# One filling quantum fewer behind each read-back of inverses, and one tile and one cadence for the modulation sums through the border, both branch projections and the output projection

## The chip, the cores and the metric

The kernel runs on one core of a Trainium2 chip. The metric is the device time of one execution in microseconds (us); of several runs the median counts.

## The reference

One layer of a bidirectional hybrid encoder, 256 tokens, width 2048, everything in f32:

```python
mod = c_act @ ada_w + ada_b                      # c_act = silu(c); six parts of 2048
shift_m, scale_m, gate_m, shift_f, scale_f, gate_f = split(mod, 6)
h = rms_norm(x) * (1 + scale_m) + shift_m
proj = h @ w_in                                  # q,k,v,gates of two branches, merge gates
y_a = (sigmoid(a_o) * rms_norm(mLSTM both ways)) @ w_branch_a
y_b = (rms_norm(gated delta rule both ways) * silu(b_z)) @ w_branch_b
x = x + gate_m * ((g_a * y_a + g_b * y_b) @ w_out)
hf = rms_norm(x) * (1 + scale_f) + shift_f
x = x + gate_f * ((silu(hf @ w_gate) * (hf @ w_up)) @ w_down)
return rms_norm(x) * norm_final_w
```

The gated delta rule (GDN) has 16 heads. For each chunk it needs the inverse of a unit triangular matrix. The mLSTM has 4 heads.

## The kernel before, in words

**Products.** Each weight is loaded as f32 (`raw`), and split into a high part `wh` (ScalarE, ACT) and a low part `wl` (VectorE, DVE, `wl = raw - wh`). TensorE (PE) adds three products. A `tjob` (line 197) makes 512 output columns: eight *quanta*, each one half (`k0`) of a 1 MB load `raw`, with one `wh`, one `wl` and 12 matmuls of 512 columns. An `fjob` (line 173) makes 128 output columns in two quanta of 24 matmuls of 256. `raw`, `wh` and `wl` have three buffers each, so the split of a quantum runs two quanta ahead of PE.

**Filling.** `rest` (line 392) lists projection jobs that nothing urgent waits for: `v`, then `mb`, `o`, `a`, `ma` groups 0 to 3. `fill(n)` issues n quanta of the list. They are set between the links of the GDN chains, whose matmuls are short and wait for one another.

**GDN.** Heads go in four groups g of four. `invert(g)` makes the inverses of a group on DVE (`gdn_invert`, lines 704 and 710, tiles `uu`, `utmp`), stores them to DRAM (`inv_d`, line 696, issued by POOL), and `gdn_blocks` reads them back as `cg` (line 723, POOL). The main loop then issues `fill(8)` (line 1029), so that the filling covers this trip, and next the transposition of `cg` (line 725) and the mixing into `R` (lines 729, 730) on DVE. `gdn_phase2` handles two heads at once in nine steps; the last ones are the output product `po` (lines 829 to 834), the normalization `on` (squares on ACT, line 857; root, line 862; DVE, lines 858 to 868) and the transposition `px` on PE (line 841), which ACT copies to `obt` (line 845) and stores to DRAM (`ob_d`, line 846). For the pair p = 1 of group 3 `px` ends the GDN part.

**Border.** Then the memory of the GDN part is given free. `o_load` (line 1076) reads the four groups of `ob_d` back, `o_split` makes `obh` and `obl` (lines 1080, 1081). The first two mLSTM heads (`cores`) run their denominators `pden` (line 962) and numerators `ph` (line 978). Next come the projection of branch B (`y_b`, tiles `yb`) with the two other heads between its quanta, that of branch A (`y_a`, tiles `ya`), and the output projection (`o_job`, tiles `o`, four groups g of 512 columns). In `o_job(3)` the last quarter is done token by token (`by_token`, lines 257 to 259), since its end releases the second norm.

**Modulation sums.** Parts 2 to 5 of `mod` are 16 sums each. `ask` (line 111) loads a 1 MB row tile `ada` on SP's queue, `add` (line 120) is one DVE instruction of 128 x 2048 (line 124) with the sum as its accumulator. Parts 2, 3 and 4 (48 sums) start with the first GDN group; part 4 (`scale_f`) is needed at the end of the output projection for `affn` (line 1313). `pump` (line 157), called once a quantum, sets them: with `room` of one tile it adds when the tile was asked for more than two quanta ago and a sum is owed (every `every[0]` quanta), and asks for the next a quantum later, so that with `every` at 1 a sum comes each four quanta; `held` keeps sums off the first steps of a pair. With `room` of three tiles (pool `sr`) each owed sum is one call of `sums`, which first fills all three tiles and then adds one.

Before, `every` is 0 from the border until the last two mLSTM heads, 1 there, and 4 with three tiles in `y_a`. In `o_job` it is 0, and `sums()` is called after quanta (4, 7), (2, 5), (2, 5) and (0, 2) of the four groups; after quantum 4 of the last one `sums(P)` adds all that are left.

Of the kernel before, what the change touches and what calls it, by code (L numbers as in the profile page):

```python
# [9 lines left out]
F32 = mybir.dt.float32  # L10
# [5 lines left out]
P = 128  # L16
T = 256
D = 2048
# [34 lines left out]
def hybrid_block(ctx: ExitStack, tc: tile.TileContext, xr, nfr, crow, pk_d, cst_d, ada2, ada4, win0, winb, wint, wba, wbb, wo, wgu, wd, out, dbg=None):  # L53
# [3 lines left out]
    def pool(stack, name, bufs=1, **kw):  # L57
        return stack.enter_context(tc.tile_pool(name=name, bufs=bufs, **kw))
# [3 lines left out]
    rows_p = pool(ctx, "rows")  # L62
# [9 lines left out]
    def order(ins, yes=True):  # L72

        return tc.keep_in_program_order(ins) if yes else ins
# [30 lines left out]
        order(S.activation(row_c[:, g * 512 : (g + 1) * 512], pc_, AF.Silu))  # L105


    room = [(rows_p, "ada", 1, 1)]
    asked, unasked, age = [], [], [0]

    def ask():

        pl, tag, bufs, _ = room[0]
        part, b = unasked.pop(0)
        raw = pl.tile([P, D], F32, tag=tag, bufs=bufs, name=f"ada{part}_{b}")
        order(nc.sync.dma_start(raw, ada4[part - 2, b]))
        asked.append((part, b, raw))
        age[0] = 0

    def add():  # L120

        part, b, raw = asked.pop(0)
        c = part * KB + b
        order(V.scalar_tensor_tensor(raw, raw, 1.0, row_c[:, :D], ALU.mult, ALU.mult, accum_out=mod[:, c : c + 1]))  # L124
        if b == KB - 1:
            c = slice(part * KB, part * KB + KB)
            V.tensor_tensor(mod[:, c], mod[:, c], pk[:, PK_ADAB + c.start : PK_ADAB + c.stop], ALU.add)
# [11 lines left out]
    def settle(keep=0, only=None):  # L139

        now = [f for f in behind if only is None or f.__name__ == only]
        for f in now[: len(now) - keep]:
            behind.remove(f)
            f()

    count, every = [0], [0]
    owed, held = [0], [False]

    def sums(n=1):

        while n and (unasked or asked):
            while unasked and len(asked) < room[0][3]:
                ask()
            add()
            n -= 1

    def pump():
        count[0] += 1
        age[0] += 1
        if every[0] and count[0] % every[0] == 0:  # L160
            owed[0] = 1
        if room[0][3] > 1:
            if owed[0]:
                owed[0] = 0
                sums()
        elif asked:
            if owed[0] and age[0] > 2 and not held[0]:
                owed[0] = 0
                add()
        elif unasked and every[0]:  # L170
            ask()
# [97 lines left out]
    def fill(n=1):  # L269

        while n and fills:
            if next(fills[0], None):
                n -= 1
            else:
                fills.pop(0)
# [217 lines left out]
    with ExitStack() as s0:  # L493
# [35 lines left out]
        ra, raw = loads(0)  # L529
# [18 lines left out]
        for b in range(KB):  # L548
            if b:
                ra, raw = loads(b)  # L550
# [475 lines left out]
    for g in range(4):  # L1026
        blocks = gdn_blocks(g)
        next(blocks)
        fill(8)
        next(blocks)  # L1030
        fill(1)
        pairs = [gdn_phase2(g, p) for p in range(2)]
        if g == 3:
            settle()
            sf.close()
            mq["pool"] = pool(sq_, "mq", side="right")
            first2 = [mlstm(h) for h in range(2)]
            for c in first2:
                next(c)
        every[0] = 1  # L1040
        for p in range(2):
            pieces = stream(4 * g + 2 * p + 4)
            for n in range(1, 10):

                held[0] = n < 4
                if p == 0:
                    next(blocks, None)
                next(pairs[p], None)
                if g == 3 and n == (8, 4)[p]:
                    next(first2[p])  # L1050
                for _ in range(last[n] if g == 3 else second[n] if p else after[n]):
                    next(pieces)
            for _ in pairs[p]:
                pass

            if g < 3:
                while 4 * g + 2 * p + 5 not in heads:
                    next(pieces)
        if g < 3:
            fills.insert(0, z_job(g + 1))  # L1060
            every[0] = owed[0] = 0
            invert(g + 1)
# [55 lines left out]
            yield from y_b(g)  # L1118

    o4s = [o_load(g) for g in range(2)]  # L1120
    every[0] = owed[0] = 0
    cores = steps(*first2)
    fill(1)
    next(cores)
# [19 lines left out]
    o_split(3, o4s[3])  # L1144
    fill(2)
    drive(cores, 3)
    every[0] = 1
    drive(steps(mlstm(2), mlstm(3)), 3)
    fill(1000)
    mgh, mgl = big(bigC, F32R, "mgh"), big(bigC, F32R, "mgl")  # L1150
    sm_.close()
    sr_ = ExitStack()
    if asked:
        add()
    room[0] = (pool(sr_, "sr"), "sr", 3, 3)
    gm = room[0][0].tile([P, D], F32, name="gm")
    dgs = {}

    def row_diag(part, g, rp):
        ms = mods[:, part == 5]  # L1160
        if not g:
            m = mod[:, part * KB : (part + 1) * KB]
            V.tensor_copy(ms[:, 0], m)
            V.tensor_tensor(ms[:, 1], m, ms[:, 0].bitcast(F32), ALU.subtract)
        dg = dgs[part, g] = rp.tile([P, 2, 4, P], F32R, tag="dg", bufs=2, name=f"dg{part}_{g}")
        for i in range(2):
            V.tensor_tensor(
                dg[:, i], ident.unsqueeze(1).broadcast_to([P, 4, P]),
                ms[:, i, 4 * g : 4 * g + 4].bitcast(F32).unsqueeze(2).broadcast_to([P, 4, P]), ALU.mult,
            )  # L1170
# [6 lines left out]
            PE.matmul(pr, onesr, woven(dg[:, i]), start=i == 0, stop=i == 1)  # L1177
        S.activation(woven(dst[:, g * 512 : (g + 1) * 512]), pr.rearrange("p (c h) -> p c h", h=2), AF.Copy)

    every[0] = 4  # L1180
    for g in range(4):
        for i, _ in enumerate(y_a(g)):
            if g and i == 3:
                merged(g - 1, mgh, mgl)
            if i in (1, 5) and g < 2:
                row_diag(2, 2 * g + i // 4, room[0][0])
            if i in (3, 7) and g < 2:
                row_spread(2, 2 * g + i // 4, gm)
    every[0] = 0


    def o_job(g, front=None):
# [112 lines left out]
    for g in range(4):  # L1305
        if g == 3:
            root()
        for i, _ in enumerate(o_job(g, front_o if g == 3 else None) if g else o_first, 0 if g else 2):
            if i in ((4, 7), (2, 5), (2, 5), (0, 2))[g]:
                sums()  # L1310
            if g == 3 and i == 4:
                sums(P)
                V.scalar_tensor_tensor(
                    affn, mod[:, 4 * KB : 5 * KB], 1.0, pk[:, PK_NFFN : PK_NFFN + KB], ALU.add, ALU.mult
                )
    if dbg is not None and "x1" in dbg:
        G.dma_start(dbg["x1"], x1)
    room[0] = (rows_p, "ada", 1, 1)
    ada_parts(5)
    sw.close()  # L1320
    sr_.close()
# [73 lines left out]
    for j in range(FB // 4):  # L1395
# [4 lines left out]
        for e2 in range(2):  # L1400
            px = gps(f"pxf{j}_{e2}")
            for e in range(2):
                f = 2 * e2 + e
                for t in range(2):
                    PE.transpose(px[:, e * T + t * P : e * T + (t + 1) * P], sg[:, t, f * P : (f + 1) * P], ident)
            b = 4 * j + 2 * e2
# [156 lines left out]
```

## Time and profile before

| what | us |
|---|---|
| median of 3 runs (1970.23 to 1975.39) | 1972.22 |
| the profiled execution's own time | 1972.89 |
| its span, first to last instruction | 1970.8 |
| PE busy in the span | 1929.8 |
| DVE busy | 1405.4 |
| ACT busy | 1025.8 |

The profile is of one execution. Its times count from the span's start. A matmul's end is modelled and overlaps the next one's start, so a busy PE is read by when its matmuls start. An f32 matmul with f32 operands stands as two records.

### The profile page before, as it was taken

To read this page: it belongs to the slowest core of one execution; us is meant where nothing else is said; L and a number is where in the kernel's file an instruction comes from. 1 tells how busy PE (TensorE), PEld (TensorE's weight loads), DVE (VectorE), ACT (ScalarE), POOL (GpSimd) and SP (SyncE) were. 2 spreads that over 40 slices of the span, in tenths; PEclk is the share of its full clock that TensorE was granted. 3 is DMA by queue.
4 is the path that set the end of the run, shared out by engine and by line. 5 is a ranking of instruction groups with operands and counts; after the bars stand their busy time and mean duration, and the time that the engine had idled before them with its cause. 6 is when DMAs were issued, how large, how long until landed. Compare 5 with 4: busy or idle time off the path is not lost.

```text
span 1970.8 us, 27090 instructions
## 1 busy us (share of the span) xinstructions
PE 1929.8 (98%) x10418; PEld 1705.2 (87%) x10418; DVE 1405.4 (71%) x2067; ACT 1025.8 (52%) x1551; POOL 116.6 (6%) x211
## 2 busy tenths in 40 slices
PE   8999999999999999999999999999999999999998
PEld 6878889998999899889787888788888888888886
DVE  6779886887788788866577878866665665555554
ACT  3137646765776577565534444644444444444444
POOL 0001210111011101110100000200000000000000
PEclk9999999999999999999899999999999999999999
DMA  9987676667576766686776888576676665565553
GB/s 399 420 349 233 182 255 241 217 221 235 213 219 214 243 209 219 208 293 244 242 296 247 343 301 333 206 255 236 241 268 239 235 239 207 195 214 199 207 199 143
DMA packets 78962, 485.64 MB, mean 246 GB/s; under 512 B 10585, under 2 KB 15969, under 8 KB 24433
## 3 DMA queue, kind: packets, MB, share of 16 engines
q1 hardware_dynamic: 63216, 450.69, 62.6%
q0 software_dynamic: 8160, 17.88, 4.4%
q10 hardware_dynamic: 7458, 15.36, 2.0%
q8 instruction: 81, 1.33, 0.3%
q14 instruction: 47, 0.39, 0.1%
HBM read 467.07 MB, written 16.82 MB: 246 GB/s over the span
## 4 chain that ended last, share of the span: by engine, by line
PE 85%; DVE 6%; DMA 5%; ACT 2%; issue 1%; SPq 0%; ACTq 0%; DVEq 0%
PE acc_gt L234 4%; PE acc_gt L235 4%; PE acc_gt L236 4%; PE acc_up L234 4%; PE acc_up L235 4%; PE acc_up L236 4%; PE acc_d L234 4%; PE acc_d L236 4%; PE acc_d L235 4%; DMA ra<-ada 3%; PE acc_b L187 2%; PE acc_b L189 2%; PE acc_o L236 2%; PE acc_b L188 2%; PE acc_o L234 2%; PE acc_o L235 2%
## 5 line engine op out<-in xcount | busy, mean ns | idle before, releaser
L215 DVE TENSOR_TENSOR wl_d<-raw_d,wh_d 128x1024 fp32r<-128x1024 f32 x88 | 107.7, 1224 | 105.9 <-ACT wh_d L213 105.9
L215 DVE TENSOR_TENSOR wl_up<-raw_up,wh_up 128x1024 fp32r<-128x1024 f32 x88 | 107.6, 1224 | 100.2 <-ACT wh_up L213 100.1
L215 DVE TENSOR_TENSOR wl_gt<-raw_gt,wh_gt 128x1024 fp32r<-128x1024 f32 x88 | 108.1, 1229 | 79.4 <-ACT wh_gt L213 79.4
L187 PE MATMUL acc_b<-hh,wh_b 128*128 128x256 f32 x576 | 162.8, 283 | 0.0
L189 PE MATMUL acc_b<-hh,wl_b 128*128 128x256 f32 x576 | 159.4, 277 | 0.1
L188 PE MATMUL acc_b<-hl,wh_b 128*128 128x256 f32 x576 | 159.1, 276 | 0.0
L213 ACT ACTIVATE wh_d<-raw_d 128x1024 fp32r<-128x1024 f32 x88 | 92.9, 1056 | 126.3 <-PE acc_d L235 118.9
L213 ACT ACTIVATE wh_gt<-raw_gt 128x1024 fp32r<-128x1024 f32 x88 | 92.9, 1056 | 121.2 <-PE acc_gt L235 71.0
L213 ACT ACTIVATE wh_up<-raw_up 128x1024 fp32r<-128x1024 f32 x88 | 92.8, 1056 | 108.1 <-PE acc_up L235 77.1
L124 DVE SCALAR_TENSOR_TENSOR ada<-ada,crow 128x2048 f32<-128x2048 f32 x64 | 145.9, 2283 | 0.0
L234 PE MATMUL acc_gt<-wh_gt,hfh 128*128 128x512 f32 x352 | 135.9, 386 | 0.0
L235 PE MATMUL acc_gt<-wh_gt,hfl 128*128 128x512 f32 x352 | 135.1, 384 | 0.0
L236 PE MATMUL acc_gt<-wl_gt,hfh 128*128 128x512 f32 x352 | 134.2, 381 | 0.0
L234 PE MATMUL acc_up<-wh_up,hfh 128*128 128x512 f32 x352 | 133.4, 379 | 0.0
L235 PE MATMUL acc_up<-wh_up,hfl 128*128 128x512 f32 x352 | 133.4, 379 | 0.0
L236 PE MATMUL acc_up<-wl_up,hfh 128*128 128x512 f32 x352 | 133.4, 379 | 0.0
L234 PE MATMUL acc_d<-wh_d,ffh 128*128 128x512 f32 x344 | 130.5, 379 | 0.0
L235 PE MATMUL acc_d<-wh_d,ffl 128*128 128x512 f32 x344 | 130.5, 379 | 0.0
L236 PE MATMUL acc_d<-wl_d,ffh 128*128 128x512 f32 x344 | 130.4, 379 | 0.0
L561 PE MATMUL first<-x,raw 128*128 128x256 f32 x512 | 114.5, 382 | 7.4 <-ACT x L555 7.0
L561 PEld LDWEIGHTS first<-x,raw 128*128 128x128 f32 x512 | 96.0, 190 | 25.9 <-ACT x L555 12.6
L188 PEld LDWEIGHTS acc_b<-hl,wh_b 128*128 128x128 f32 x576 | 111.3, 193 | 0.1
(382 smaller groups left out, 5262.1 us busy)
## 6 DMA issues: line engine op xcount, KB each, us to landing
ada<-ada SPq DMA_DIRECT2D x64, 1024.0 KB, 6.2
raw_gt<-wgu SPq DMA_DIRECT2D x44, 1024.0 KB, 4.9
raw_up<-wgu SPq DMA_DIRECT2D x44, 1024.0 KB, 4.9
raw_d<-wd SPq DMA_DIRECT2D x44, 1024.0 KB, 4.9
raw_b<-winb SPq DMA_DIRECT2D x36, 1024.0 KB, 5.0
ra<-ada SPq DMA_DIRECT2D x32, 1025.0 KB, 15.6
raw<-win SPq DMA_DIRECT2D x16, 1024.0 KB, 14.5
raw_z<-wint SPq DMA_DIRECT2D x16, 1024.0 KB, 5.2
```

What stands on the lines that cost most here:

```text
L124: order(V.scalar_tensor_tensor(raw, raw, 1.0, row_c[:, :D], ALU.mult, ALU.mult, accum_out=mod[:, c : c + 1]))
L187: PE.matmul(o, wh[:, k], woven(hh[:, kk]), start=kk == 0, stop=False)
L188: PE.matmul(o, wh[:, k], woven(hl[:, kk]), start=False, stop=False)
L189: PE.matmul(o, wl[:, k], woven(hh[:, kk]), start=False, stop=kk == KB - 1)
L213: order(S.activation(wh, raws[u][:, k0 : k0 + 2], AF.Copy), early)
L215: order(V.tensor_tensor(wl, raws[u][:, k0 : k0 + 2], wh.bitcast(F32), ALU.subtract), early)
L234: order(PE.matmul(ps[t], xh[:, kk, c], woven(wh[:, k]), start=kk == 0, stop=False), early and steps > 1)
L235: PE.matmul(ps[t], xl[:, kk, c], woven(wh[:, k]), start=False, stop=False)
L236: PE.matmul(ps[t], xh[:, kk, c], woven(wl[:, k]), start=False, stop=kk == last)
L561: PE.matmul(first[o], raw[:, o], x[:, b], start=b == 0 and o % 2 == 0, stop=b == KB - 1 and o % 2 == 1)
```

## The change

Three things change, all in the order of the work; every product and every sum is still made.

1. After the read-back of groups 1, 2 and 3 seven quanta are issued in place of eight. What is not issued there comes later from the same list.
2. The three-tile pool `sr` for the sums goes: `room` goes, and all 48 sums go through the one tile of `rows_p`. `every` stays at 1 from GDN group 3 on, through the border (where `held` is set to false), `y_b`, `y_a` and `o_job`. The calls of `sums()` after single quanta go.
3. What is left of part 4 is summed after quantum 3 of `o_job(3)`, not after quantum 4.

```diff
-    room = [(rows_p, "ada", 1, 1)]
     asked, unasked, age = [], [], [0]
 
     def ask():
 
-        pl, tag, bufs, _ = room[0]
         part, b = unasked.pop(0)
-        raw = pl.tile([P, D], F32, tag=tag, bufs=bufs, name=f"ada{part}_{b}")
+        raw = rows_p.tile([P, D], F32, tag="ada", name=f"ada{part}_{b}")
...
         while n and (unasked or asked):
-            while unasked and len(asked) < room[0][3]:
+            if not asked:
                 ask()
             add()
...
-        if room[0][3] > 1:
-            if owed[0]:
-                owed[0] = 0
-                sums()
-        elif asked:
+        if asked:
             if owed[0] and age[0] > 2 and not held[0]:
...
-        fill(8)
+        fill(7 if g else 8)
         next(blocks)
         fill(1)
...
     o4s = [o_load(g) for g in range(2)]
-    every[0] = owed[0] = 0
+    held[0] = False
     cores = steps(*first2)
...
     drive(cores, 3)
-    every[0] = 1
     drive(steps(mlstm(2), mlstm(3)), 3)
...
-    if asked:
-        add()
-    room[0] = (pool(sr_, "sr"), "sr", 3, 3)
-    gm = room[0][0].tile([P, D], F32, name="gm")
+    sr = pool(sr_, "sr")
+    gm = sr.tile([P, D], F32, name="gm")
...
-    every[0] = 4
     for g in range(4):
         for i, _ in enumerate(y_a(g)):
...
-    every[0] = 0
...
         for i, _ in enumerate(o_job(g, front_o if g == 3 else None) if g else o_first, 0 if g else 2):
-            if i in ((4, 7), (2, 5), (2, 5), (0, 2))[g]:
-                sums()
-            if g == 3 and i == 4:
+            if g == 3 and i == 3:
+                every[0] = owed[0] = 0
                 sums(P)
...
-    room[0] = (rows_p, "ada", 1, 1)
     ada_parts(5)
```

The order in which the two programs issue their instructions shows what this does. The lines of the changed kernel are lower by 6 (lines 184 to 1100), by 11 in the residual code and by 2 in `add`.

**First place: DVE at the read-back of group 2** (`uu` ends the inversion, `cg` is the read-back, `wl_o` and `wl_b` are low parts of quanta). Before:

```order
L710 TENSOR_TENSOR uu_4939<-uu_4939,utmp_5937 64x30
L215 TENSOR_TENSOR wl_o_0_2_6342<-raw_o_0_6323,wh_o_0_2_6341 128x1024
L215 TENSOR_TENSOR wl_o_1_0_6360<-raw_o_1_6357,wh_o_1_0_6359 128x1024
L215 TENSOR_TENSOR wl_o_1_2_6376<-raw_o_1_6357,wh_o_1_2_6375 128x1024
L215 TENSOR_TENSOR wl_o_2_0_6394<-raw_o_2_6391,wh_o_2_0_6393 128x1024
L215 TENSOR_TENSOR wl_o_2_2_6410<-raw_o_2_6391,wh_o_2_2_6409 128x1024
L215 TENSOR_TENSOR wl_o_3_0_6428<-raw_o_3_6425,wh_o_3_0_6427 128x1024
L725 STREAM_TRANSPOSE cg_6296<-cg_6296 128x512
```

The same place on DVE after the change:

```order
L704 TENSOR_TENSOR uu_4908<-uu_4908,utmp_5919 64x30
L209 TENSOR_TENSOR wl_o_0_0_6326<-raw_o_0_6323,wh_o_0_0_6325 128x1024
L209 TENSOR_TENSOR wl_o_0_2_6342<-raw_o_0_6323,wh_o_0_2_6341 128x1024
L209 TENSOR_TENSOR wl_o_1_0_6360<-raw_o_1_6357,wh_o_1_0_6359 128x1024
L209 TENSOR_TENSOR wl_o_1_2_6376<-raw_o_1_6357,wh_o_1_2_6375 128x1024
L209 TENSOR_TENSOR wl_o_2_0_6394<-raw_o_2_6391,wh_o_2_0_6393 128x1024
L719 STREAM_TRANSPOSE cg_6278<-cg_6278 128x512
L723 TENSOR_SCALAR R<-cg_6278,cst 128x256
```

Between the inversion's last instruction and the transposition stand five low parts in place of six.

**Second place: PE at the end of the GDN part** (`po`, `px` of the last two heads, `acc_ma` the last job of `rest`). Before, `po` comes after the last quantum of the list, and `px` right behind it:

```order
L236 MATMUL acc_ma_1_9102<-wl_ma_3_2_9289,hh 128x512
L829 MATMUL po_1_9310<-z_1_9208,at_7688 128x128
...
L834 MATMUL po_1_9310<-z_1_9208,at_7987 128x128
L841 MATMUL px_1_9311<-cst,on_1_0_9324 128x128 x2
L962 MATMUL pden_9374<-ones,mdec_8891 128x1
L841 MATMUL px_1_9311<-cst,on_1_1_9325 128x128
L962 MATMUL pden_9374<-ones,mdec_8891 128x1 x5
```

After the change three quanta (`ma_2_2`, `ma_3_0`, `ma_3_2`) stand between `po` and `px`; this is the end of the last one and what follows:

```order
L229 MATMUL acc_ma_1_9137<-wh_ma_3_2_9322,hl 128x512
L230 MATMUL acc_ma_1_9137<-wl_ma_3_2_9323,hh 128x512
L835 MATMUL px_1_9257<-cst,on_1_0_9270 128x128 x2
L835 MATMUL px_1_9257<-cst,on_1_1_9271 128x128 x2
L956 MATMUL pden_9375<-ones,mdec_8798 128x1 x6
L956 MATMUL pden_9392<-ones,mdec_9088 128x1 x6
L972 MATMUL ph_0_0_9411<-vt_8808,mdec_8798 128x512
```

On DVE, a little later, a sum now stands in the border, behind the last `obl` and ahead of a low part of `yb` (after the change):

```order
L209 TENSOR_TENSOR wl_yb_1_2_9529<-raw_yb_1_9508,wh_yb_1_2_9528 128x1024
L1075 TENSOR_TENSOR obl<-o_3_9429,obh 128x1024
L122 TENSOR_SCALAR ada_8_9490,mod<-ada_8_9490,crow 128x2048
L209 TENSOR_TENSOR wl_yb_2_0_9548<-raw_yb_2_9545,wh_yb_2_0_9547 128x1024
L979 RECIPROCAL ssh_9406<-ssh_9406 128x2
```

Before, one `hs` of line 987 (128x512) stood there in place of the sum; that `hs` comes later now.

**Third place: DVE in the last group of the output projection** (`ada_12` to `ada_15` are sums of part 4). Before:

```order
L215 TENSOR_TENSOR wl_o_1_0_11464<-raw_o_1_11461,wh_o_1_0_11463 128x1024
L124 TENSOR_SCALAR ada_12_11376,mod<-ada_12_11376,crow 128x2048
L215 TENSOR_TENSOR wl_o_1_2_11483<-raw_o_1_11461,wh_o_1_2_11482 128x1024
L215 TENSOR_TENSOR wl_o_2_0_11501<-raw_o_2_11498,wh_o_2_0_11500 128x1024
L124 TENSOR_SCALAR ada_13_11442,mod<-ada_13_11442,crow 128x2048
L124 TENSOR_SCALAR ada_14_11479,mod<-ada_14_11479,crow 128x2048
L124 TENSOR_SCALAR ada_15_11516,mod<-ada_15_11516,crow 128x2048
L215 TENSOR_TENSOR wl_o_2_2_11524<-raw_o_2_11498,wh_o_2_2_11523 128x1024
L127 TENSOR_TENSOR mod<-mod,pk 128x16
L215 TENSOR_TENSOR wl_o_3_0_11542<-raw_o_3_11539,wh_o_3_0_11541 128x1024
```

After the change:

```order
L209 TENSOR_TENSOR wl_o_1_0_11468<-raw_o_1_11465,wh_o_1_0_11467 128x1024
L209 TENSOR_TENSOR wl_o_1_2_11484<-raw_o_1_11465,wh_o_1_2_11483 128x1024
L122 TENSOR_SCALAR ada_14_11447,mod<-ada_14_11447,crow 128x2048
L209 TENSOR_TENSOR wl_o_2_0_11508<-raw_o_2_11505,wh_o_2_0_11507 128x1024
L209 TENSOR_TENSOR wl_o_2_2_11524<-raw_o_2_11505,wh_o_2_2_11523 128x1024
L209 TENSOR_TENSOR wl_o_3_0_11542<-raw_o_3_11539,wh_o_3_0_11541 128x1024
L122 TENSOR_SCALAR ada_15_11500,mod<-ada_15_11500,crow 128x2048
L209 TENSOR_TENSOR wl_o_3_2_11546<-raw_o_3_11539,wh_o_3_2_11545 128x1024
L125 TENSOR_TENSOR mod<-mod,pk 128x16
```

Two of the sums stand earlier now, and the last one has the last two low parts around it. With one tile its load can be issued only when `ada_14` has been added; on SP's queue it stands behind the load of `raw_gt_0`.

More of the change, by code (lines that the diff above doesn't have):

```diff
@@ L1185, in hybrid_block @@
             if i in (1, 5) and g < 2:
-                row_diag(2, 2 * g + i // 4, room[0][0])
+                row_diag(2, 2 * g + i // 4, sr)
             if i in (3, 7) and g < 2:
                 row_spread(2, 2 * g + i // 4, gm)
-    every[0] = 0
     def o_job(g, front=None):
```

## The prediction

> **What bounds the kernel now.** I read the page first: busy times, then the waits of PE, then the chain of waits where they lie.
>
> ```profile
> PE 1929.8 (98%) x10418; PEld 1705.2 (87%) x10418; DVE 1405.4 (71%) x2067; ACT 1025.8 (52%) x1551; POOL 116.6 (6%) x211
> PE 85%; DVE 6%; DMA 5%; ACT 2%; issue 1%; SPq 0%; ACTq 0%; DVEq 0%
> ```
>
> PE is busy for 98% of the span and holds 85% of the chain. The change takes no matmul away, so it can only gain where PE stands still or runs at a lower clock. The waits of PE (us in total, times, longest) name two such places that the change touches:
>
> ```profile
> PE acc_o L236 <- DVE wl_o L215: 3.7, 4, 2.1
> PE px L841 <- DVE on L868: 3.6, 1, 3.6
> ```
>
> The second is the end of the GDN part. The chain there (start, us, what), the clock of three stretches (us, then busy PE, PEld, DVE, ACT, POOL, then the granted clock, DMA share, GB/s), and three rows of the same chain elsewhere:
>
> ```profile
> 951.54 0.24 PE po L834 x2
> 951.80 1.14 ACT on L857 x8
> 953.20 1.06 issue
> 955.40 0.73 PE px L841 x2
> 956.67 2.35 PE pden L962 x12
> 959.34 1.93 PE pden L962 x10
> 961.26 12.66 PE ph L978 x24
> 973.92 0.22 PE acc_yb L234
> ```
>
> ```profile
> 950.00:962.00 12.00, 8.37 (x45) 7.70 (x45) 2.88 (x9) 4.57 (x14) 0.00 (x0) 0.73 0.32 126
> 962.00:966.00 4.00, 4.00 (x6) 1.61 (x5) 0.59 (x6) 0.93 (x3) 2.59 (x4) 0.54 0.71 243
> 1022.00:1031.00 9.00, 9.00 (x47) 7.93 (x46) 5.17 (x11) 2.46 (x4) 0.00 (x0) 0.81 0.85 303
> ```
>
> ```profile
> 994.64 0.87 PE pxa L994 x8
> 1023.37 2.57 PE pden L962 x24
> 1035.51 5.15 PE ph L978 x12
> ```
>
> PE ends `po` at 951.78 and starts `px` at 955.40: it waits 3.62 us for squares, root and normalization. Behind the wait it runs at a lower clock (0.73, then 0.54). `px` and 24 `pden` take 5.86 us from 955.40 to 961.26; at full clock eight transpositions take 0.87 and 24 `pden` 2.57, 3.44 in all. The 24 `ph` take 12.66 against 2 x 5.15 = 10.30. So from `po` to the first matmul of `yb` 22.14 us pass, where 13.74 would do if nothing had to be waited for.
>
> **The change, part by part.** (a) **Border.** Three quanta, one saved behind each read-back, now stand between `po` and `px`. A quantum's pitch is seen from two low parts on DVE, one after the other:
>
> ```profile
> 674.05 1.23 DVE L215 TENSOR_TENSOR wl_o<-raw_o,wh_o 128x1024 fp32r<-128x1024 f32 x1 [1.37 <-ACT wh_o L213]
> 676.64 1.22 DVE L215 TENSOR_TENSOR wl_o<-raw_o,wh_o 128x1024 fp32r<-128x1024 f32 x1 [1.36 <-ACT wh_o L213]
> 678.71 0.71 DVE L725 STREAM_TRANSPOSE cg<-cg 128x512 f32<-128x512 f32 x1 [0.84 <-DMA cg<-inv_d]
> 680.35 1.22 DVE L215 TENSOR_TENSOR wl_o<-raw_o,wh_o 128x1024 fp32r<-128x1024 f32 x1
> ```
>
> It is 2.59 us, so the three last 7.8. What they must cover is the 3.62 of before, and what may stand ahead of the normalization on DVE now, one sum (2.28, below) and one low part (1.22): 7.1 at most. So the wait goes whole, and with it, as I take it, the low clock behind it: 3.62 + (5.86 - 3.44) + (12.66 - 10.30) = 8.40.
>
> A gap that closes shows what is late next. `yb` needs `obh` and `obl`, which come from DRAM:
>
> ```profile
> 959.37 0.84 ACT L845 ACTIVATE obt<-px,pk 128x256 f32<-128x256 f32 x2 [4.82 <-PE px L841]
> 962.63 1.51 POOL L1076 DMA_DIRECT2D o<-ob_d  x2 [55.44 <-ACT dn L964]
> 972.95 0.76 POOL L1076 DMA_DIRECT2D o<-ob_d  x1 [0.80 <-DVE obl L1081]
> 979.95 1.23 DVE L1081 TENSOR_TENSOR obl<-o,obh 128x1024 fp32r<-128x1024 f32 x1 [0.75 <-ACT obh L1080]
> 981.76 1.22 DVE L215 TENSOR_TENSOR wl_yb<-raw_yb,wh_yb 128x1024 fp32r<-128x1024 f32 x1
> ```
>
> This trip is DMA after DMA on POOL's queue (store, two loads, two more when the first are split), and a faster PE doesn't shorten it: from `obt` at 959.37 to the end of the last `obl` at 981.18 it takes 21.8. Count from the start T of `px` in the changed kernel. `obt` follows two evictions of `ma` on ACT, at about T + 1.1, so the last `obl` ends at T + 22.9. Behind it now stand the sum `ada_8` (2.28) and then the low part of quantum 4 of `yb` (1.22): T + 26.4. PE is at that low part's first product at T + 13.74 + 4 x 2.59 + 0.43 = T + 24.5. It waits 1.9. Net gain of the border 8.40 - 1.9 = **6.5**, with 8.4 as one end (trip shorter, no wait) and 3 as the other (the trip or the sum later by 3.5).
>
> On the clock: the row of 1022 to 1031 shows 0.81 with PE busy for all of its 9.00 us; no wait is there, only the thin `pden`. The Trainium skill, "TensorE: Matmul & The Clock Gate", Part 1, says that the clock falls to half after an idle window of about 3.4 us and comes back after a busy one of that length, the windows running free. The drop behind the 3.62 us wait agrees with it. A drop behind `pden`, which the profile calls busy, goes further than the page's word "idle". By the page alone the 8.40 stand; by the row at 1022 the thin `px` and `pden` of the border may bring a half-clock window again.
>
> That would cost half a window in `ph`, 1.7 us (the stretch at 0.81 lost 0.19 x 9). But PE would then reach `yb`'s quantum 4 at T + 26.2, still before T + 26.4: the sum stays at 6.5, and only the better end, 8.4, would be lost.
>
> The same sum `ada_8` and the next one, `ada_9`, crowd DVE up to 1004. DVE was idle for some 5 us there, and the two take 4.6. I take 0.5 as lost, between 0 and 3.
>
> (b) **Last group of the output projection.** Rows of before on DVE, and PE's wait on it:
>
> ```profile
> 1238.27 2.28 DVE L124 SCALAR_TENSOR_TENSOR ada<-ada,crow 128x2048 f32<-128x2048 f32 x1
> 1240.48 2.29 DVE L124 SCALAR_TENSOR_TENSOR ada<-ada,crow 128x2048 f32<-128x2048 f32 x1
> 1242.69 2.29 DVE L124 SCALAR_TENSOR_TENSOR ada<-ada,crow 128x2048 f32<-128x2048 f32 x1
> 1244.91 1.22 DVE L215 TENSOR_TENSOR wl_o<-raw_o,wh_o 128x1024 fp32r<-128x1024 f32 x1
> ```
>
> ```profile
> L236 PE MATMUL acc_o<-wl_o,mgh 128*128 128x512 f32 x120 | 45.4, 381 | 2.4 <-DVE wl_o L215 2.4
> ```
>
> Three sums in a row hold the next low part up to 1244.91, and PE loses 2.4 us on the low parts of this stage (all groups). In this group DVE had eight low parts (9.8), the residual (2.6) and five sums (11.4), 23.8 in eight quanta of 20.7; with two sums it has 17.0. New is a wait on DVE: `ada_15` can be asked for only when `ada_14` is added. Let the group start at 0. The low part before `ada_14` waits for a buffer (2.6) and its high part (1.06): 4.9 at its end, `ada_14` ends at 7.2. The load lands in 6.2 (median of the page):
>
> ```profile
> ada<-ada SPq DMA_DIRECT2D x64, 1024.0 KB, 6.2
> ```
>
> So `ada_15` ends at 15.7 and the last low part, queued behind it on DVE, at 16.9. PE needs that at 6 x 2.59 + 1.3 + 0.4 = 17.2. It just fits; I take 0.3 as lost. Gain **2.1**. One end is 2.4; the other a loss of 3, when the load takes 5 us more.
>
> (c) **Seven quanta behind the read-back.** In group 2 DVE already waits there (0.84, first fence of this part): `cg` landed when the transposition starts, at 678.71, so it can't start earlier. The low part of 676.64 now comes behind the transposition and most of the mixing: at 680.35, ending at 681.57. Its high part was set by PE's third quantum before:
>
> ```profile
> 675.55 1.06 ACT L213 ACTIVATE wh_o<-raw_o 128x1024 fp32r<-128x1024 f32 x1 [1.53 <-PE acc_o L235]
> 861.73 0.71 DVE L725 STREAM_TRANSPOSE cg<-cg 128x512 f32<-128x512 f32 x1 [0.71 <-DMA bc<-mal_d]
> ```
>
> The quantum thus starts at about 675.8 + 2 x 2.59 = 681.0 and uses the low part at 681.4: 0.2 late. Group 3 waits by the same arithmetic (0.71 at 861.73). Group 1 had no wait. I take **0.5** for all, between 0 and 5.2, a whole quantum twice.
>
> (d) **The rest.** Quanta shift against the chains of groups 1 to 3, and ACT loads two more function tables there (1.28 each), where it is a third idle. `y_a` and the first output groups had almost no wait, and have as many sums. PE's idle time in the stretches of groups 2 to 3 bounds this:
>
> ```profile
> 470.00:655.00 185.00, 181.63 (x1307) 171.15 (x1306) 154.69 (x301) 121.63 (x226) 20.35 (x40) 1.00 0.67 219
> 655.00:838.00 183.00, 180.09 (x1301) 170.19 (x1300) 150.61 (x297) 120.01 (x225) 18.78 (x36) 1.00 0.66 220
> ```
>
> Some 6 us are idle in 368; I take no change, and 3 to either side.
>
> Sum: 6.5 - 0.5 + 2.1 - 0.5 = 7.6 less. The profiled execution took 1972.89 us around its span of 1970.8, 0.7 above the median of 1972.22. 1972.89 - 7.6 = **1965.3**.
>
> **Rivals.** *The border's trip decides.* The first `obl` leaves PE about 1 us of room, and each of the four loads from DRAM could be later, since the weights of `yb` and the sums now ask for the same queues at that time. Then of 8.4 some 5 come back as waits for `obh`, `obl` and low parts: 1972.89 - 3.4 - 2.1 + 1 + 1 = 1969.4. For it: DVE and DMA were already waited for at each `obl`. Against it: the same loads in the same order.
>
> *The read-back is late.* With seven quanta a `cg` that lands a quantum later stops PE for 2.6 us, and if the clock falls, for 1.7 more; in groups 2 and 3 that is 8.6, which eats the gain: 1973.9. Against it: `cg` landed no more than 0.84 after DVE was ready, with eight.
>
> *One tile is too few (slower).* With one tile the load of a sum is issued when the sum before has ended, and the next sum comes four quanta later, 10.4 - 2.3 = 8.1 us. A load that takes longer stops DVE, and low parts queue behind it; 24 sums from the border on stand like this. PE has about 1 us of room. To end 5.9 us slower the 24 must lose 7.6 + 5.9, 0.56 each, so the loads would have to take 9.7 on average: 1979 and more. For it: three tiles hid the load entirely. Against it, the row of this stretch:
>
> ```profile
> ada<-ada SPq DMA_DIRECT2D x24, 1024.0 KB, 6.3
> ```
>
> That the change doesn't do what it says is bounded by the order: three quanta do stand between `po` and `px`.
>
> **How the numbers follow.** Forecast 0.66, the border's trip 0.20, the read-back 0.08, one tile 0.06. A difference of 0.3% (5.9 us, to 1966.3) is about what a measurement of this kernel tells from none. Of the forecast 0.56 lies below 1966.3 and 0.10 above, since the bounds of the border alone reach from 8.4 to 3; of the first rival 0.02 lies below. Faster 0.58, same 0.36, slower 0.06. The range goes from 1960.0 (border 8.4, output 2.4, nothing lost, 2 from the chains of the groups) to 1972.5 (the first rival with 3 lost in the groups); the two last rivals mostly lie outside.
>
> **What would show it.** The wait of `px` for `on` is gone and `po` to `yb` takes about 14 us besides the three quanta; the granted clock stays near 1.00 there. PE waits once for `wl_yb` in quantum 4, 1 to 3 us. The wait of `acc_o` for `wl_o` falls from 3.7 to below 1.8. DVE waits for `cg` in groups 2 and 3 for 3 us, PE for almost nothing. Wrong would be: waits of DVE for `ada` loads, waits of PE for `obh` above 2 us, a clock below 0.9 at the read-backs.

## The result and the profile after

| | us |
|---|---|
| before, median of 22 runs | 1973.45 (1970.23 to 1977.56) |
| after, median of 22 runs | 1969.99 (1967.75 to 1975.22) |
| ratio | 0.9985, 95% interval 0.9979 to 0.9991 |
| after, the profiled execution: its own time, its span | 1972.23, 1970.2 |

The change made the kernel 3.0 us faster (1.8 to 4.1 by the interval), where 7.6 had been forecast. Differences below are such ratios times 1973 us, their intervals in brackets; a ratio is estimated from all the runs, so it is not quite the quotient of the medians, which lie 3.5 us apart here. The profiled execution of after lies 2.2 us above its own median, so the two spans hardly differ; where the time went is read by stages.

The busy times of after and four of PE's waits (us in total, times, longest):

```profile
PE 1926.1 (98%) x10418; PEld 1701.1 (86%) x10418; DVE 1405.9 (71%) x2067; ACT 1028.4 (52%) x1553; POOL 116.5 (6%) x211
```

```profile
PE acc_yb L230 <- DVE wl_yb L209: 3.5, 3, 1.6
...
PE ph L972 <- ACT dn L958: 2.7, 1, 2.7
PE pxa L988 <- DVE hal L993: 2.3, 1, 2.3
PE acc_o L230 <- DVE wl_o L209: 1.9, 3, 1.2
```

The wait of `px` (3.6) is gone. Three waits are new: for `dn`, for low parts of `yb`, for `hal`. To see what they cost, take points of the program at which PE has issued the same matmuls in both kernels, and compare when it gets there in the two profiled executions (us from the span's start):

| PE starts | before | after | after minus before |
|---|---|---|---|
| a matmul behind the read-back of group 1 | 603.04 | 604.44 | +1.40 |
| the last read-back's end (group 3) | 859.15 | 860.84 | +1.68 |
| the sixth `ph` | 965.53 | 958.63 | -6.90 |
| the seventh `ph` | 966.03 | 961.92 | -4.11 |
| first low part in `yb` | 974.19 | 970.48 | -3.71 |
| `yb`, quantum 3 | 981.96 | 979.00 | -2.96 |
| `yb`, quantum 4 | 984.55 | 983.48 | -1.07 |
| behind the sum `ada_9` | 995.78 | 996.27 | +0.48 |
| second batch of `pxa` | 997.24 | 1000.13 | +2.89 |
| output projection, group 1 | 1197.06 | 1199.79 | +2.72 |
| its last token part | 1250.60 | 1250.94 | +0.34 |

Of the first +1.40, 1.31 is there at 227 us, before the programs differ. The border gains 8.6 us (+1.68 to -6.90), as the 8.40 of the forecast had it. Then it is all given back, and 1.2 more, in 42 us: 2.8 at `dn`, 3.0 on the way to quantum 4, 1.5 and 2.4 behind `ada_9`. Only the last group of the output projection keeps its 2.4.

**Where the first 2.8 go.** The border of after on the engines (start, us, engine, what, idle time before it and what ended it; a queue's row is the issue):

```profile
953.37 0.60 PE L835 MATMUL px<-cst,on 128*128 128x128 f32 x4
...
954.16 0.48 ACT L839 ACTIVATE obt<-px,pk 128x256 f32<-128x256 f32 x1
954.30 0.33 ACTq L350 DMA_DIRECT2D ma_d<-ev_ma  x1
954.72 0.39 ACTq L840 DMA_DIRECT2D ob_d<-obt  x1
...
961.69 0.24 ACT L958 ACTIVATE dn<-pden 128x4 f32<-128x4 f32 x2 [5.12 <-DMA ob_d<-obt]
...
961.92 1.55 PE L972 MATMUL ph<-vt,mdec 128*128 128x512 f32 x3 [2.70 <-ACT dn L958]
...
962.21 1.51 POOL L1070 DMA_DIRECT2D o<-ob_d  x2 [61.30 <-ACT dn L958]
```

`dn` waits until the store of `obt` has landed (its releaser is that DMA; `dn` lies in a pool that is opened where the GDN part's memory was given free, which is read from the code). So do the loads of `o`. The issues of that stretch, with size and median us to landing, after and then before:

```profile
raw_yb<-wbb SPq DMA_DIRECT2D x1, 1024.0 KB, 6.4
...
ma_d<-ev_ma ACTq DMA_DIRECT2D x1, 512.0 KB, 6.5
ob_d<-obt ACTq DMA_DIRECT2D x2, 128.0 KB, 6.5
```

```profile
ob_d<-obt ACTq DMA_DIRECT2D x2, 128.0 KB, 1.7
```

The same store takes 6.5 us in place of 1.7: the three quanta brought their own load of weights and the store of their job's result right ahead of it. PE reached `px` 2.0 us sooner than before, but the loads of `o` go out at 962.21, before at 962.63.

**Where the rest goes.** DVE in `yb`, after; then the stretch 978 to 1000 of after and of before (us, then busy PE, PEld, DVE, ACT, POOL, granted clock, DMA share, GB/s):

```profile
978.86 1.22 DVE L1075 TENSOR_TENSOR obl<-o,obh 128x1024 fp32r<-128x1024 f32 x1
980.00 2.28 DVE L122 SCALAR_TENSOR_TENSOR ada<-ada,crow 128x2048 f32<-128x2048 f32 x1
...
982.21 1.22 DVE L209 TENSOR_TENSOR wl_yb<-raw_yb,wh_yb 128x1024 fp32r<-128x1024 f32 x1
...
992.77 2.29 DVE L122 SCALAR_TENSOR_TENSOR ada<-ada,crow 128x2048 f32<-128x2048 f32 x1 [4.55 <-DMA ada<-ada]
...
994.99 2.36 DVE L209 TENSOR_TENSOR wl_yb<-raw_yb,wh_yb 128x1024 fp32r<-128x1024 f32 x2
...
999.59 1.65 DVE L993 SCALAR_TENSOR_TENSOR hal<-pxa,pk,hah 128x256 fp32r<-128x256 f32 x4
```

```profile
978.00:1000.00 22.00, 16.34 (x76) 13.07 (x75) 17.45 (x20) 9.28 (x13) 0.56 (x2) 1.00 0.99 376
```

```profile
978.00:1000.00 22.00, 22.00 (x111) 19.11 (x110) 16.14 (x22) 12.10 (x17) 1.61 (x4) 1.00 0.92 349
```

The sum `ada_8` stands ahead of a low part, as forecast: 1.9 of the 3.0 us on the way to quantum 4. The other 1.1 go at the start of `yb` (0.4) and at a late low part of quantum 3 (0.75). The sum `ada_9` is worse: its load takes 10.4 us (issued at 982.32, landed at 992.75), DVE stands still for 4.55 with low parts and `hal` queued behind. The DMA engines are at 0.99 there. Before, PE was busy for all of the 22.00 us; now for 16.34.

### The profile page after: what moved, and what is told of

It is laid out like the page before. It is cut to its first block, busy times and chain, and to the rows that moved or that the text cites. A ratio compares the mean times of both kernels' runs of the same rounds, so it can differ in the third digit from the quotient of the medians.

```text
span 1970.2 us, 27078 instructions
## 1 busy us (share of the span) xinstructions
PE 1926.1 (98%) x10418; PEld 1701.1 (86%) x10418; DVE 1405.9 (71%) x2067; ACT 1028.4 (52%) x1553; POOL 116.5 (6%) x211
## 5 line engine op out<-in xcount | busy, mean ns | idle before, releaser
L181 PEld LDWEIGHTS acc_b<-hh,wh_b 128*128 128x128 f32 x576 | 111.4, 193 | 0.1
```

Source lines behind the costliest of these rows:

```text
L181: PE.matmul(o, wh[:, k], woven(hh[:, kk]), start=kk == 0, stop=False)
```

## The experiments

My theory after this reading: the border's gain is real, and it is given back because `ob_d` lands late and because two sums, their loads above all, crowd a stretch in which DMA was nearly full already. The main rival: `yb` is bound by its weights' loads, and whatever comes sooner to it waits there.

**Part 1 alone** (`e1_fill7_alone`), the kernel before with

```diff
-        fill(8)
+        fill(7 if g else 8)
```

> Part 1 alone: the kernel before with seven quanta behind the read-backs of groups 1 to 3; the sums stay off in the first half of the border and keep their three tiles later. Theory (the border gains 8.6 us up to the first `ph`, gives back 2.8 at the `dn` wait, and the rest is lost because two sums and their 1 MB loads crowd `yb`): without these sums some 5 of the 8.6 stay, so 1968 to 1969 beside 1973.4 for the kernel before, -4.5 to -5.5. The DMA share in the stretch 980 to 990 falls below 0.95. Rival (the loads of weights and of the branch output bound `yb` by themselves, whoever adds to them): the gain is stalled away all the same, -1.5 to 0.

Measured 1972.24 us, -0.8 (-2.6 to +0.8): the expectation failed. So did its sign: the DMA share from 980 to 990 is 1.02, not below 0.95. Its waits, and two stretches:

```profile
PE acc_ya L236 <- DVE wl_ya L215: 3.2, 2, 2.2
...
PE ph L978 <- ACT dn L964: 2.3, 1, 2.3
PE pxa L994 <- DVE hal L999: 1.7, 1, 1.7
```

```profile
958.00:970.00 12.00, 9.72 (x20) 3.96 (x19) 2.95 (x10) 3.39 (x8) 2.59 (x4) 0.86 0.80 286
...
980.00:990.00 10.00, 10.00 (x48) 8.77 (x47) 6.65 (x8) 3.39 (x4) 0.53 (x1) 1.00 1.02 373
```

By the same points of the program it gains 8.6 to the sixth `ph`, loses 2.4 at `dn` and 1.8 to a lower clock behind that wait (0.86 here, 1.00 in the profile of after, behind waits of 2.3 and 2.7). Up to `pxa` 2.7 are left. They are gone by the output projection; in `y_a` PE waits 3.2 us for low parts (before: none). DVE there:

```profile
1077.97 2.28 DVE L124 SCALAR_TENSOR_TENSOR ada<-ada,crow 128x2048 f32<-128x2048 f32 x1
...
1080.18 2.28 DVE L124 SCALAR_TENSOR_TENSOR ada<-ada,crow 128x2048 f32<-128x2048 f32 x1
...
1082.40 2.28 DVE L124 SCALAR_TENSOR_TENSOR ada<-ada,crow 128x2048 f32<-128x2048 f32 x1
...
1084.61 1.22 DVE L215 TENSOR_TENSOR wl_ya<-raw_ya,wh_ya 128x1024 fp32r<-128x1024 f32 x1
```

Three sums stand in a row ahead of a low part; in before the same three start 9 and 11 us apart. The count of quanta that sets them is another one now.

**Parts 2 and 3 alone** (`e2_sums_alone`), the changed kernel with `fill(8)`.

> Parts 2 and 3 alone: the changed kernel with eight quanta at every read-back. Theory: the last group of the output projection gains its 2.4 to 2.8; the border keeps the 3.6 us wait of `px`, `ob_d` is stored with nothing ahead of it (lands 1.8 us after its issue), and PE comes to `yb` later, so the sums there cost 0.5 to 1.5: -1 to -2.3 in all beside the kernel before. Rival (the sums cost nothing, the weights' loads bound `yb`): -2.5. A loss of over 1 us would say that the sums in the border cost by DVE's order alone, with PE's time of arrival no part of it.

Measured 1972.71 us, -0.2 (-1.8 to +1.6), less than either forecast. The sums in `yb` cost 0.5 by the points of the program, as expected. Two waits:

```profile
PE pxn L1323 <- ACT xn L1261: 4.5, 1, 4.5
PE px L835 <- DVE on L862: 4.0, 1, 4.0
```

The output projection's last group gains 2.4, and 2.7 are lost right behind it: the count of quanta is another one, so the last sum stands at 1250.81, among the residual's instructions, and the second norm waits 4.5 in place of 1.8. Neither part alone is worth what both are together: -0.8 and -0.2 against -3.0.

**`px` one quantum earlier** (`e3_px_earlier`): the changed kernel, two quanta between `po` and `px` and the third behind it.

```diff
-                for _ in range(last[n] if g == 3 else second[n] if p else after[n]):
+                for _ in range((last if p == 0 else (0, 1, 2, 1, 2, 2, 1, 1, 2, 1))[n] if g == 3 else second[n] if p else after[n]):
```

> The changed kernel with two of the three quanta between `po` and `px` and the third one behind `px`, so that `ob_d` is stored ahead of `ma_d` on ACT's queue and a quantum stands between `px` and `pden`. Theory (`ob_d` lands 6.5 us after its issue because `ma_d` stands ahead of it, `dn` and the loads of `o` wait for that): the stores land in under 2.5 us, the `dn` wait of 2.7 goes, and the first loads of `o` are out 2 to 5 us sooner as seen from `px`: 2.5 to 5 better than the changed kernel, -6 to -8 beside the kernel before. Rival (`yb` is bound by its loads): the stall only moves from `ph` into `yb`, -3 to -4, as the changed kernel.

Measured 1970.03 us, -4.1 (-5.9 to -2.4). The store of `ob_d`, and the stretch 954 to 960:

```profile
ob_d<-obt ACTq DMA_DIRECT2D x2, 128.0 KB, 1.8
```

```profile
954.00:960.00 6.00, 6.00 (x23) 3.46 (x23) 0.68 (x6) 1.63 (x5) 2.60 (x4) 0.72 0.97 299
```

The store lands in 1.8 us and PE no longer waits for `dn`: that half of the theory held. The time is the rival's: a lower clock takes part of it at once (0.72, PE busy for all of the 6.00 us), and of the 6.0 us by which PE then leads the kernel before, all are gone by 999. The stall moved into `yb`.

**No sums in the border and `yb`** (`e4_no_border_sums`): the changed kernel, `every` at 0 from the border to the last two mLSTM heads, and `add` allowed a quantum earlier (`pace`) from `y_a` on, to catch up.

```diff
-    owed, held = [0], [False]
+    owed, held, pace = [0], [False], [2]
...
-            if owed[0] and age[0] > 2 and not held[0]:
+            if owed[0] and age[0] > pace[0] and not held[0]:
...
+    every[0] = owed[0] = 0
     held[0] = False
...
     drive(cores, 3)
+    every[0] = 1
...
+    pace[0] = 1
     for g in range(4):
         for i, _ in enumerate(y_a(g)):
```

> The changed kernel with no sum between the border and the last two mLSTM heads, as before the change, and a sum each three quanta in place of four from `y_a` on, to catch up; one tile throughout. Theory (the sum ahead of a low part of `yb`, and the next one, whose load takes 10.4 us, cost PE 1.8, 1.4 and 2.5 us): 4 to 5.5 better than the changed kernel, -7 to -9 beside the kernel before, and nothing lost in `y_a`. Rival (the weights' loads bound `yb`): within 1 us of the changed kernel. A second way to fail: three quanta are too few for one tile, DVE waits some 1 us per sum for loads in `y_a` and PE loses 1 to 3 there.

Measured 1980.02 us, +7.7 (+5.3 to +10.1).

```profile
PE acc_o L230 <- DVE wl_o L209: 9.5, 4, 5.6
PE acc_ya L230 <- DVE wl_ya L209: 2.7, 3, 1.4
```

At `pxa` it was 2.9 ahead of the kernel before, counted from the last read-back, where the changed one is 1.2 behind: 4.1 between the two, as expected. (No sum is added in `yb` here, but with `every` at 1 again the load of the next one is issued there, at 981.02.) Then a sum each three quanta lost 13 us in `y_a` and the output projection: the second way to fail, and larger than I had put it.

**Without the loads of two sums** (`e5_no_loads`), and **with all loads and short instructions** (`e6_small_adds`), both from the changed kernel:

```diff
-        order(nc.sync.dma_start(raw, ada4[part - 2, b]))
+        if part != 3 or b not in (9, 10):
+            order(nc.sync.dma_start(raw, ada4[part - 2, b]))
...
-        order(V.scalar_tensor_tensor(raw, raw, 1.0, row_c[:, :D], ...
+        src = row_c[:, :D] if part == 3 and b in (9, 10) else raw
+        order(V.scalar_tensor_tensor(raw, src, 1.0, row_c[:, :D], ...
```

```diff
+        w = P if part == 3 and b in (8, 9, 10) else D
-        order(V.scalar_tensor_tensor(raw, raw, 1.0, row_c[:, :D], ...
+        order(V.scalar_tensor_tensor(raw[:, :w], raw[:, :w], 1.0, row_c[:, :w], ...
```

The first leaves two sums out of the result, the second makes three of them from 128 of 2048 columns.

> The changed kernel without the loads of the two sums whose tiles are asked for in the border and in `yb` (`ada_9` and `ada_10` of the second part summed); both DVE instructions stay, with the same length, on another operand, so those two sums are left out of the result. 2 MB less pass in a stretch with a DMA share of 0.99. Theory A (the loads crowd the DMA engines; DVE waits 4.6 us for `ada_9` and the low parts and `hal` queue behind it): the waits 1.4 and 2.5 of PE go, 3 to 4 less than the changed kernel, -6 to -7.5 beside the kernel before. Theory B (the DVE time of the sums alone crowds): at most 0.7 less than the changed kernel, -3 to -4.

> The changed kernel with all loads, but with the instructions of the three sums of the border and of `yb` (`ada_8`, `ada_9`, `ada_10`) cut from 2048 to 128 columns, so that these sums are incomplete. Theory A (loads): only the 1.8 us of `ada_8`, whose load had long landed, comes back; `ada_9` still waits for its load and holds the low part: -4 to -5.5 beside the kernel before. Theory B (DVE time): 1.8 and some 2 to 3 more, -6.5 to -8.

Measured 1966.89 us without the loads, -6.1 (-8.7 to -3.7), and 1971.07 with short instructions, -1.6 (-3.4 to +0.2). The sum `ada_9` in the one and in the other:

```profile
988.07 2.29 DVE L124 SCALAR_TENSOR_TENSOR ada<-crow 128x2048 f32<-128x2048 f32 x1
```

```profile
993.14 0.29 DVE L123 SCALAR_TENSOR_TENSOR ada<-ada,crow 128x128 f32<-128x128 f32 x1 [6.09 <-DMA ada<-ada]
```

Theory A: 2 MB fewer give 3 us more than the changed kernel has, and the waits for `hal` and the low part behind `ada_9` are gone, although DVE works as long. With 0.29 us of DVE's work left in place of 2.28, DVE still stands for 6.09 until the load is there. So the price of `ada_9` is not its work, it is that DVE waits for its load with the low parts behind it; whether the bytes of the load cost by themselves, these two don't tell. The 1.9 us of `ada_8`, which theory A too had expected back, are gone at their place, and at the second batch of `pxa` this run is 1.2 better than the changed kernel by the points of the program; its time does not show it (-1.6 against -3.0, with intervals that overlap).

**Sums later** (`e7_sums_later`): as in `e4`, but a sum each three quanta only with the last two mLSTM heads and in the first two groups of `y_a`.

```diff
     drive(cores, 3)
+    every[0] = 1
+    pace[0] = 1
     drive(steps(mlstm(2), mlstm(3)), 3)
...
     for g in range(4):
+        pace[0] = 1 if g < 2 else 2
```

> A full kernel: the changed one with no sum from the border to the last two mLSTM heads, and a sum each three quanta in place of four from there through the first two groups of `y_a`, four again behind that, so that the last sums stand where the changed kernel has them. The run with three quanta through all of `y_a` and the output projection kept 4 us more in the border and lost 9 later. Theory (sums in `yb` cost, and three quanta suffice where the mLSTM steps stretch the quanta): -5 to -7 beside the kernel before. If one tile can't take a sum each three quanta anywhere, the 4 us are lost again: -3 or less.

Measured 1967.36 us, -5.5 (-7.9 to -3.2). **The same with `px` one quantum earlier** (`e8_later_px_earlier`):

> The same with `px` one quantum earlier, so that `ob_d` is stored ahead of `ma_d`. Theory (two causes that add up): the `dn` wait and the late loads of `o` go too, 1 to 3 less than with the sums alone moved, -7 to -9 beside the kernel before. Rival (one budget of DMA in `yb`, on which both draw): no more than with the sums alone moved.

Measured 1963.34 us, -8.7 (-11.0 to -6.3): faster than both kernels. What is left of the waits in `yb`, the stretch 978 to 1000, and the load of a sum that is issued in it, with that sum:

```profile
PE acc_yb L230 <- DVE wl_yb L209: 0.8, 1, 0.8
```

```profile
978.00:1000.00 22.00, 22.00 (x111) 19.10 (x110) 16.15 (x22) 10.55 (x17) 0.53 (x1) 1.00 0.94 378
```

```profile
ada<-ada SPq DMA_DIRECT2D x1, 1024.0 KB, 10.8
```

```profile
1002.21 2.29 DVE L122 SCALAR_TENSOR_TENSOR ada<-ada,crow 128x2048 f32<-128x2048 f32 x1
```

PE is busy for all of the stretch again, at a DMA share of 0.94 and with as many bytes moved as in after (378 and 376 GB/s). One 1 MB load of a sum is in it here too, issued at 981.73 and as slow as that of `ada_9` (10.8 us); `e1`, `e4` and `e7` have one as well (12.5, 12.3 and 11.1). What is gone is the DVE instruction that waited for it: the sum stands at 1002.21, behind the landing, and no low part queues behind a wait. So "their loads above all" in my theory holds for the wait; that the bytes cost by themselves is not shown. The run with `px` earlier alone differs from this one by the sums: from quantum 4 of `yb` to the second batch of `pxa` it loses 2.8, this one nothing.

The main rival falls for this kernel, but not everywhere. In `e1` (and in `e4`, with 4.70) the weights of `yb` are late by themselves:

```profile
990.61 2.00 ACT L213 ACTIVATE wh_yb<-raw_yb 128x1024 fp32r<-128x1024 f32 x2 [4.65 <-DMA raw_yb<-wbb]
```

The low parts are late with them, `hal` stands behind those on DVE, and PE waits 1.7 us for it. Here ACT waits 2.6 at that place and PE does not.

**The store on POOL's queue** (`e9_store_by_pool` from the changed kernel, `e10_later_by_pool` from the one with the sums later):

```diff
-            S.dma_start(ob_d[g][hl_], obt)
+            (G if g == 3 and p else S).dma_start(ob_d[g][hl_], obt)
```

> The changed kernel with the two last stores of `ob_d` issued on POOL's queue, which is idle then, in place of ACT's, where `ma_d` stands ahead; the place of `px` stays. If the order on ACT's queue is what makes them land 6.5 us after their issue, they land in under 3, the wait for `dn` (2.7) goes and the first loads of `o` are out 3 us sooner; the run with `px` earlier showed that most of this is given back in `yb` while the two sums are there, so -4 to -5 beside the kernel before. If the DMA engines are what is shared (`raw_yb`, 1 MB, is under way at the same time), the stores still take 5 or more, and the time is that of the changed kernel, -3 to -3.5.

> The same store on POOL's queue with the sums moved out of the border and `yb` (as in the run of that name, which gave -5.5). If the order on the queue is the cause: -7.5 to -9.5, as with `px` earlier (-8.7). If the engines are shared: -5 to -6.

Measured 1969.54 us, -2.8 (-4.5 to -1.0), and 1965.67, -6.9 (-9.5 to -4.3). The stores of the first:

```profile
ob_d<-obt POOLq DMA_DIRECT2D x2, 128.0 KB, 6.0
```

They take 6.0 us on an idle queue too. That the order on ACT's queue was the cause, as the expectation of `e3` had it, fell. The -6.9 of the second is between its two forecasts; its trace has the same late store (5.8) and the same wait for `dn`, and its interval overlaps that of -5.5, so it says nothing more.

**Eight quanta with the sums later** (`e11_later_eight`): `e7` with `fill(8)`.

> The kernel with the sums moved out of the border and `yb`, but with eight quanta at every read-back: what part 1 is worth where no sum crowds `yb`. Theory (the three quanta between `po` and `px` are worth 8.6, less 2.7 at `dn`, less 1 to 2 in `yb`): this one is 4 to 5 slower than with seven, -0.5 to -2.5 beside the kernel before, from the output projection. Rival (the gain of the moved sums has nothing to do with part 1): -5 or better.

Measured 1971.83 us, -1.4 (-3.2 to +0.4). So part 1 is worth 4.1 where no sum crowds `yb` (-5.5 against -1.4), as expected. Up to the second batch of `pxa` the traces show 3.6 of it. Behind that the two differ in more than the border: the sums stand at other quanta, and DVE waits 14.6 us for `ada` here, 3.1 in `e7`.

**`ma_d` stored last** (`e12_later_ma_d_last`): `e7`, the store of the last job issued behind the two of `ob_d`, on ACT's queue.

```diff
-            S.dma_start(dst, ev)
+            if name == "ma3":
+                late.append((dst, ev))
+            else:
+                S.dma_start(dst, ev)
...
             for _ in pairs[p]:
                 pass
+            if g == 3 and p:
+                S.dma_start(*late[0])
```

> The kernel with the sums moved out of the border and `yb`, on ACT's queue as before, but the store `ma_d` of the last job is issued behind the two of `ob_d`; `raw_yb` (1 MB) is still under way at that time. POOL's queue had not helped (6.2 us), so the engines are shared; this tells by which transfer. If the 512 KB of `ma_d` ahead are the cause, `ob_d` lands in 1.7 to 3 us, the `dn` wait (2.7) goes, and the time is -7 to -9 beside the kernel before. If the 1 MB of `raw_yb` is, the stores take 4 to 6 and the time stays near -5.5.

Measured 1965.27 us, -7.3 (-9.9 to -4.7).

```profile
ob_d<-obt ACTq DMA_DIRECT2D x2, 128.0 KB, 4.1
```

Both transfers count. With only `raw_yb` ahead the first of the two stores takes 4.1 and lands at 955.42, 0.4 behind `raw_yb` (955.01); with `ma_d` ahead as well it takes 5.9 to 6.5 and lands 0.3 to 0.4 behind `ma_d`; with neither, 1.7. The store is as the second forecast had it and the time as the first, since at 4.1 PE loses only 0.3 at `dn`.

## Why the prediction was right and wrong

The direction and the two gains were right; what gives the first one back was not, and with it the size, 7.6 forecast and 3.0 measured. **The step that failed** is the one in part (a) that gives back 1.9 at a low part and takes "0.5 as lost" for the two sums: 2.4 of the 8.40 were to come back, and in the profiled executions 9.8 did. In its place stand 2.8 at `dn`, 3.0 up to quantum 4 of `yb` and 4.0 behind `ada_9`: a late store, and a wait of DVE for a load, where only DVE's work had been counted.

- *Wait and clock at `px`, 8.40:* 8.6 in the trace. The wait is gone in every trace with quanta between `po` and `px`: right. (The eight transpositions of the sum are four: 0.43 us from the first `px` to the first `pden` in after, where 0.87 had been counted.) The clock of after stays at 1.00, the first two rows; that is luck of this execution. Over the 14 us from `px` on it is 0.88 in nine of the ten other traces with seven quanta, and 0.76 in the tenth (`e6`). The third row is of `e9`, which waits as long at `dn`. So the low-clock stretch that the prediction priced at 1.7 us does come in these ten (0.12 x 14 = 1.7).

```profile
950.00:958.00 8.00, 8.00 (x49) 6.77 (x48) 2.98 (x3) 5.21 (x7) 0.00 (x0) 1.00 0.69 219
958.00:970.00 12.00, 9.30 (x22) 3.72 (x20) 3.21 (x9) 4.49 (x11) 2.59 (x4) 1.00 0.79 294
```

```profile
958.00:970.00 12.00, 9.45 (x20) 4.29 (x21) 4.03 (x10) 5.34 (x12) 3.10 (x5) 0.86 0.78 285
```

- *"A faster PE doesn't shorten it", the trip of 21.8 from `obt` to the last `obl`:* the trip got longer. `obt` came at T + 0.8 and the last `obl` ended at 980.08, T + 26.7 in place of T + 22.9. I had moved a store to a place behind three quanta and had left out their DMAs: `ma_d` had landed 5.8 us before the store was issued, and no weights were under way; now 1.5 MB are. From `px` to `yb` (first matmul at 969.35) 16.0 us pass in place of 13.74, 2.7 of them the wait for `dn`, which I had not in the sum: in before its wait for the same store lay behind `ph` at a low clock.
- *The low part behind `ada_8`, 1.9:* 1.9 by the table. The size is right by two errors that cancel: low part and PE were both late, by some 3.7 us.
- *The two sums, 0.5 with 3 as the far end:* 4.0 behind `ada_9`. I priced them in DVE time alone, 4.6 us of work in 5 idle ones. DVE's wait for the load of `ada_9` was the price: without the load it goes (`e5`), with a short instruction it stays (`e6`), and with the sum behind the landing the same load costs PE nothing (`e8`).
- *Output projection, 2.1:* 2.4. The wait for its low parts fell from 2.4 to

```profile
L230 PE MATMUL acc_o<-wl_o,mgh 128*128 128x512 f32 x120 | 45.4, 381 | 0.2 <-DVE wl_o L209 0.2
```

 All waits of `acc_o`, with those of the filling job of that name, fell from 3.7 to 1.9, where below 1.8 had been put. The load of `ada_15` did arrive in time here; in `e2`, with another count of quanta, the same cadence cost 2.7.
- *Read-backs, 0.5, and DVE's waits for `cg`, 3 us in groups 2 and 3:* DVE waits longer than that,

```profile
DVE cg L719 <- DMA cg<-inv_d: 4.6, 2, 3.0
DVE cg L719 <- DMA bc<-mal_d: 3.9, 1, 3.9
```

 and PE loses next to nothing by it: between 603 and 859 us, 0.3 in after, 2.1 in `e1`, -0.4 to 1.3 in the nine others with seven quanta. Right in the sum. The waits of PE at the read-backs that the table of waits shows (2.8 for `wl_mb`) are won back within the group.
- *The rival "the border's trip decides", 1969.4 at 0.20:* the time came out near it, 1970.0, and its reason holds in part: transfers land later because weights and sums ask for DMA at the same time. Its terms do not, so the nearness is in part luck. It looked for loads of `o` that take longer and for waits at `obh` and `obl`; the first two loads took 5.6 and 6.3 us (before, 6.1), and what came late was the store ahead of them and the load of `ada_9`. Against it I had put "the same loads in the same order"; a load of weights and the store `ma_d` now stand ahead of them. *One tile too few:* its mechanism happened, at one sum: the load of `ada_9` took 10.4 us, more than the 8.1 between two sums, and low parts queued behind the wait. Its size did not: DVE waits for `ada` twice (4.6 and 2.5), PE pays for the first. No run has a second tile there, so whether one would have hidden that load is not shown.

What stays open: how much of the late weights in `e1` and `e4` (1.7 us at `hal`) is due to the load of a sum that is under way beside them; and whether the 2 us by which both parts together (-3.0) beat the sum of the single ones (-1.0) are more than chance, since the intervals reach over them.

## What to carry to other kernels

When work is moved in front of a store or a load, move its DMAs along in the estimate: what counts for a small store is how many bytes are under way when it is issued, not on which queue it stands. Before a gap on the main engine is closed, look at how long the loads take in the stretch that will then start sooner: here those of 1 MB issued from 978 to 985 took 8 to 9 us before and 10 to 11 after, and 8.6 us gained came back as 9.8 of waits. And a side job in that stretch is priced by when its load lands, not by the length of its instruction: what stands behind it on the same engine waits too. Placed behind the landing, the same load cost nothing (`e8`).

## What the runs showed of the hardware

At the end of the GDN part the first store of 128 KB lands 0.3 to 0.4 us behind the transfers that were issued ahead of it, on its own queue or another: after 1.7 us with none, 4.1 behind 1 MB, 5.9 to 6.5 behind 1.5 MB, also from POOL's idle queue (`e9`, `e10`). The Trainium skill, "DMA: Bandwidth & Descriptors", section "Issuing engines are not separate DMA queues", says that all run on the same 16 engines and interleave; that they share agrees, but no interleaving helped the small store, which landed last.

The clock falls behind thin matmuls without a wait: 0.72 over 954 to 960 in `e3`, PE busy for 6.00 of 6.00 us. A wait of 2.7 us at `dn` left it at 1.00 from 958 to 970 in after, and at 0.86 over the same 12 us in `e9`: equal waits, without and with a fall. The Trainium skill, "TensorE: Matmul & The Clock Gate", Part 1, has windows that run free, which agrees with the second; the first goes further than its word "idle".
